# A streaming-encoder block on one core: both banded score products with 128 rows, and the final norm's roots in groups

## The chip, the core and the metric

The kernel runs on one core of a Trainium2 chip. The metric is device time in microseconds (us) from the start to the end of one execution. Engines: PE (TensorE, matmuls), DVE (VectorE), ACT (ScalarE), POOL (GpSimd) and SP (SyncE, which here only issues transfers). Each engine works through its own queue in order; SP, ACT and POOL also issue DMA transfers from their queues.

## What is computed

One layer on 1024 tokens of width 1024: an adaptive norm, a combined projection, two attention branches (latent attention, and banded attention of chunks of 64 tokens over their own and 8 earlier chunks), gates, an output projection, then a mixture of 32 experts (two per token) and a final norm. The parts that the change touches, cut from the reference:

```python
def rms_norm(x, g):
    y = xf * lax.rsqrt(jnp.mean(xf * xf, axis=-1, keepdims=True) + NORM_EPS)
    return y * g

def one_chunk(n):          # banded branch: 8 heads of 64, chunks of 64
    qc = q[n * 64 : n * 64 + 64]; kb, vb = the 9 chunks up to n
    sc = einsum('bqhd,bkhd->bhqk', qc, kb) * d ** -0.5 + bias
    p = softmax(where(valid, sc, NEG_INF))
    return einsum('bhqk,bkhd->bqhd', p, vb)
...
merged = sigmoid(gate_a) * (o_a @ w_oa) + sigmoid(gate_b) * (o_b @ w_ob)
x = x + gt1 * (merged @ w_out)
x = x + gt2 * hierarchical_moe(...)
return rms_norm(x, g_final)
```

## The kernel before

**Precision.** A float32 operand is split into a high part (rounded to the matmul format fp32r by a ScalarE copy) and a low part (the rest, by a DVE subtraction); `split`, lines 65 to 68. A product is then three matmuls, high x high, high x low, low x high (`mm3`, lines 70 to 74).

**Stages.** `front` (0 to some 206 us in the trace) norms, projects the latents and values, and stores the latent queries. `attend` runs 32 units of the banded branch, then 32 of the latent branch; `merge` blends the branches, projects out, routes the tokens; `experts` runs the experts and ends with the final norm.

**A unit** is one head and a group of two 128-token blocks (`unit`, from line 508). `soft` computes the scores of a block into PSUM (`st`, two buffers), adds the bias and takes the row minimum on DVE (L554), takes the exponential on ACT (L561), and scales by the reciprocal sum on POOL (L563). `trans` transposes the probabilities on PE (L578) and splits them; `value` multiplies by the values (L589, L590), adds the two halves through the tile o (L593, L594), splits the sum (L596, L597) and stores it. `pipeline` interleaves: unit i computes scores while unit i - 2 transposes and unit i - 3 multiplies by the values.

**Fill.** Between these steps a generator `fill` advances PE work of another kind. In the banded half that is `project`: a list of jobs, each 128 output columns of the combined projection for all 1024 tokens in 16 steps of three 512-column matmuls (two halves of 8 steps, an evacuation after each half). 33 steps run ahead of unit 0, then 10.8 with each unit (`BAND_RATE`). The list is pair 0 (queries, keys), pair 1, gates 0 to 3, pair 2, gates 4 to 7, pair 3, gates 8 to 15. A pair is two heads; units 8p to 8p + 7 belong to pair p, the even head (r = 0) in the first four for pairs 0 to 2.

**Banded scores.** `evac_q` puts the high part of a head's 64 query rows on one half of 128 partitions and the low part on the other (tile q). `evac_k` puts the high part of the keys on both halves (kd: L722 on ACT for one, L723 on POOL for the other) and the low part on the half of the head's own rows alone (kl, L724). So the first product (L785) has 128 rows and gives (high + low query) x high key, and the second one 64 rows:

```python
nc.tensor.matmul(out, it["q"][:, r, qs], it["kd"][:, r, ks], start=True, stop=False)
nc.tensor.matmul(out, it["q"][rr, r, qs], it["kl"][rr, ks], start=False, stop=True)
```

The latent branch takes its scores by `mm3` with 96 or 128 rows.

**Expert weights** come in loads of 1024 KB (tile we) on SP's queue; from the fourth on, each waits for the load two before it to have landed, and for its buffer (`weights`, L1292). Rows of ACT and DVE that split them are L67 and L68 with the tile whl.

**Pools.** s8 has 18 buffers of 8 KB per partition, s4 has 10 of 4 KB, s2 has 6 of 2 KB; t1 holds o and ohl.

**Final norm** (lines 1366 to 1392): g_final is loaded as one row, spread to 128 rows by matmuls with ones (L1371) and scaled on ACT (L1372). The residual rows are read back in eight tiles xz. For each, ACT squares with a row sum (L1385), DVE makes the root by a seed and three Newton steps on 128x1 (`rsqrt`, lines 76 to 92, eight small instructions), and the tile is multiplied by root and g_final on DVE (L1391); tiles 1 and 4 (`ASIDE`) by ACT (L1388) and POOL (L1389). SP stores it (L1392).

A scheduler puts the instructions of each engine in its queue, so their order is not quite that of the code.

## Time and profile before

| | us |
|---|---|
| median of 3 runs | 1348.7 (1345.55 to 1357.09) |
| the profiled execution | 1343.9 |
| its span, first to last instruction | 1342.2 |
| PE, DVE, ACT, POOL busy | 1216.0, 857.1, 642.4, 404.0 |

All times of rows are of the profiled execution, counted from its span's start. A matmul's end is modelled and overlaps the next one; what a matmul costs in a stream is read from start to start.

### The profile page before, as it was taken

To read this page: it belongs to the slowest core of one execution; us is meant where nothing else is said; L and a number is where in the kernel's file an instruction comes from. 1 tells how busy PE (TensorE), PEld (TensorE's weight loads), DVE (VectorE), ACT (ScalarE), POOL (GpSimd) and SP (SyncE) were. 2 spreads that over 40 slices of the span, in tenths; PEclk is the share of its full clock that TensorE was granted. 3 is DMA by queue.
4 is the path that set the end of the run, shared out by engine and by line. 5 is a ranking of instruction groups with operands and counts; after the bars stand their busy time and mean duration, and the time that the engine had idled before them with its cause. 6 is when DMAs were issued, how large, how long until landed. Compare 5 with 4: busy or idle time off the path is not lost. (4 is left out here: it accounts for less than half of the span.)

```text
span 1342.2 us, 17715 instructions
## 1 busy us (share of the span) xinstructions
PE 1216.0 (91%) x5866; PEld 958.7 (71%) x5866; DVE 857.1 (64%) x1761; ACT 642.4 (48%) x1271; POOL 404.0 (30%) x439
## 2 busy tenths in 40 slices
PE   4899969999999999999979999998599999998980
PEld 3787847677777777788869988887476776665640
DVE  7974525547556434367868872666787787875746
ACT  7453414334443344455667861312466565554533
POOL 3320203222222222222335755533323322322221
PEclk9899979999999999999989999999699999998995
DMA  9245791345355223389866574678589888999956
GB/s 370 90 127 187 214 294 61 104 143 190 93 165 179 69 84 118 126 271 313 256 202 194 173 223 160 234 299 330 179 278 292 295 294 295 304 317 321 311 180 258
DMA packets 103238, 288.36 MB, mean 215 GB/s; under 512 B 16629, under 2 KB 35189, under 8 KB 88776
## 3 DMA queue, kind: packets, MB, share of 16 engines
q1 hardware_dynamic: 85800, 247.32, 54.1%
q0 software_dynamic: 10288, 23.10, 6.9%
q10 hardware_dynamic: 7056, 16.78, 3.4%
q8 instruction: 47, 0.77, 0.2%
q14 instruction: 47, 0.39, 0.1%
HBM read 235.74 MB, written 68.17 MB: 226 GB/s over the span
## 5 line engine op out<-in xcount | busy, mean ns | idle before, releaser
L68 DVE TENSOR_TENSOR whl<-we,whl 128x1024 fp32r<-128x1024 f32 x125 | 150.6, 1222 | 49.8 <-ACT whl L67 46.7
L72 PE MATMUL bank<-hh,wx 128*128 128x512 f32 x384 | 159.1, 414 | 13.4 <-ACT wx L67 13.4
L563 POOL TENSOR_SCALAR pr<-pr,total 128x640 f32<-128x640 f32 (+7 forms) x128 | 96.1, 755 | 226.5 <-DVE total L562 189.7
L67 ACT CAST whl<-we 128x1024 fp32r<-128x1024 f32 x125 | 129.3, 1053 | 69.5 <-PE pp L74 53.2
L73 PE MATMUL bank<-hl,wx 128*128 128x512 f32 x384 | 152.3, 397 | 0.0
L74 PE MATMUL bank<-hh,wx 128*128 128x512 f32 x384 | 152.0, 397 | 0.0
L561 ACT ACTIVATE pr<-st,lowest 128x640 f32<-128x640 f32 (+7 forms) x128 | 89.8, 703 | 87.7 <-DVE lowest L554 51.3
L1396 POOL DMA_INDIRECT scratch_x<-eo,idx x32 | 57.7, 1803 | 213.9 <-DMA scratch_x<-eo,idx 72.8
L72 PE MATMUL pp<-whl,xh 128*128 128x512 f32 x256 | 113.3, 443 | 4.3 <-ACT whl L67 4.3
L1535 PE MATMUL pp<-we,hT 128*128 128x512 f32 x248 | 114.1, 602 | 0.8 <-ACT hT L1522 0.8
L68 DVE TENSOR_TENSOR pl<-bank,ph 128x512 fp32r<-128x512 f32 (+1 forms) x152 | 91.3, 613 | 32.1 <-ACT ph L67 28.2
L73 PE MATMUL pp<-whl,xh 128*128 128x512 f32 x256 | 104.8, 409 | 3.2 <-DVE whl L68 3.1
L74 PE MATMUL pp<-whl,xl 128*128 128x512 f32 x256 | 101.6, 397 | 0.0
L597 POOL TENSOR_TENSOR ohl<-o,ohl 64x256 fp32r<-64x256 f32 x64 | 54.4, 850 | 142.9 <-ACT ohl L596 92.8
L72 PEld LDWEIGHTS bank<-hh,wx 128*128 128x128 f32 x384 | 72.9, 190 | 33.0 <-ACT wx L67 13.8
L67 ACT CAST ph<-bank 128x512 fp32r<-128x512 f32 (+1 forms) x152 | 77.9, 530 | 36.3 <-PE bank L578 29.9
L74 PEld LDWEIGHTS bank<-hh,wx 128*128 128x128 f32 x384 | 72.7, 189 | 16.6 <-issue 0.5
L578 PE MATMUL bank<-ident,pr 128*128 128x128 f32 x528 | 82.8, 277 | 0.0
L73 PEld LDWEIGHTS bank<-hl,wx 128*128 128x128 f32 x384 | 73.2, 191 | 12.7 <-issue 0.2
L1535 PEld LDWEIGHTS pp<-we,hT 128*128 128x128 f32 x248 | 46.8, 193 | 48.1 <-issue 39.5
L554 DVE CUSTOM_DVE_ANT_0 st<-st,bias 128x640 f32<-128x640 f32 (+2 forms) x64 | 42.0, 666 | 49.0 <-PE st L786 48.8
L578 PEld LDWEIGHTS bank<-ident,pr 128*128 128x128 f32 x528 | 61.5, 142 | 5.5 <-issue 0.5
(380 smaller groups left out, 2905.1 us busy)
## 6 DMA issues: line engine op xcount, KB each, us to landing
we<-in_w_e SPq DMA_DIRECT2D x85, 1024.0 KB, 8.5
mw<-in_w_ada SPq DMA_DIRECT2D x64, 256.0 KB, 3.4
we<-in_w_e SPq DMA_DIRECT2D x17, 512.0 KB, 6.9
x<-in_x SPq DMA_DIRECT2D x16, 512.0 KB, 4.6
wada<-in_w_mod SPq DMA_DIRECT2D x8, 1024.0 KB, 8.9
w<-in_w_g SPq DMA_DIRECT2D x16, 512.0 KB
scratch_gate<-gs ACTq DMA_DIRECT2D x32, 256.0 KB, 3.0
gt<-scratch_gate SPq DMA_DIRECT2D x32, 256.0 KB, 2.9
```

What stands on the lines that cost most here:

```text
L67: nc.scalar.copy(hi, src)
L68: (eng or nc.vector).tensor_sub(lo, src, hi.bitcast(F32))
L72: mm(ps, lh, rh, start=start, stop=False)
L73: mm(ps, lh, rl, start=False, stop=False)
L74: mm(ps, ll, rh, start=False, stop=stop)
L554: nc.vector.tensor_tensor_reduce(sv, sv, bv, op0=OP.add, op1=OP.min, scale=1.0, scalar=3e38, accum_out=lowest)
L561: nc.scalar.activation(pv, sv, AF.Exp, bias=lowest, scale=-1.0, accum_out=total)
L563: nc.gpsimd.tensor_scalar(pr[:, 0:w], pr[:, 0:w], total, 1.0, op0=OP.mult, op1=OP.mult)
L578: nc.tensor.transpose(tp[:, i * P:(i + 1) * P], probs[s][:, lc:lc + P], self.ident)
L597: nc.gpsimd.tensor_sub(hl[rows, 1], o[rows, 1], hl[rows, 0].bitcast(F32))
L1396: self.nc.gpsimd.indirect_dma_start(out=self.scratch["x1"], out_offset=bass.IndirectOffsetOnAxis(ap=rows, axis=0), in_=o, in_offset=None, ...
L1535: nc.tensor.matmul(po[n], hT[:, ks], w[:, ns], start=k == 0, stop=k == 1)
```

## The change

Banded scores: the keys' low part gets a tile for each head of the pair, filled on both halves (the head's own by DVE, the other by a ScalarE copy, new L725), and the second product uses all 128 rows. It then also adds low query x low key. The even head's tile comes from t1 with one buffer, the odd head's from s4. The tile o shrinks to one half, one buffer, written in place. The list of jobs becomes pair 0, gates 0 and 1, pair 1, gates 2 to 5, pair 2, gates 6 to 8, pair 3, gates 9 to 15.

Final norm: g_final is read to 128 rows by one transfer into an s8 tile, ahead of the last expert's scatter in the code, and scaled on ACT. The squares of tiles 0 and 1, 2 to 4, 5 to 7 share one root chain each (eleven small instructions on 128x2 or 128x3), and all eight tiles are multiplied on DVE.

```diff
-ASIDE = (1, 4)
+FINAL = ((0, 2), (2, 5), (5, 8))
...
-            o = self.t1.tile([P, 2, 256], F32, name="o")
-            nc.scalar.copy(o[rows, 0], po[other, 0:256])
-            nc.vector.tensor_add(o[rows, 1], po[rows, 0:256], o[rows, 0])
+            o = self.t1.tile([P, 256], F32, name="o", bufs=1)
+            nc.scalar.copy(o[rows], po[other, 0:256])
+            nc.vector.tensor_add(o[rows], po[rows, 0:256], o[rows])
...
-                it["kl"] = self.t4([P, S], F32R, "kl")
+                it["kl"] = [self.t1.tile([P, S], F32R, name="kl", bufs=1), self.t4([P, S], F32R, "kl")]
...
-                    nc.vector.tensor_sub(kl[top, cs], pf[top], kd[top, r, cs].bitcast(F32))
+                    nc.vector.tensor_sub(kl[r][top, cs], pf[top], kd[top, r, cs].bitcast(F32))
+                    nc.scalar.copy(kl[r][low, cs], kl[r][top, cs].bitcast(F32))
...
-        jobs = pair_jobs(0)
-        for p in range(1, 4):
-            jobs += pair_jobs(p)
-            jobs += [gate(n) for n in range(4 * p - 4, 4 * p)]
-        jobs += [gate(n) for n in range(12, 16)]
+        jobs, gates = pair_jobs(0), iter(range(16))
+        for p, n in ((1, 2), (2, 4), (3, 3)):
+            jobs += [gate(next(gates)) for _ in range(n)] + pair_jobs(p)
+        jobs += [gate(n) for n in gates]
...
-                nc.tensor.matmul(out, it["q"][rr, r, qs], it["kl"][rr, ks], start=False, stop=True)
+                nc.tensor.matmul(out, it["q"][:, r, qs], it["kl"][r][:, ks], start=False, stop=True)
...
+        gf = self.t8([P, D], F32, "gf")
+        src = a["g_final"]
+        nc.sync.dma_start(gf, bass.AP(tensor=src.tensor, offset=src.offset, ap=[[0, P], [1, D]]))
         scatter(E - 1, self.down(self.turn_hidden(hid), lambda c: self.whole(E - 1, c)))
-        gf = self.t4([P, D], F32, "gf")
-        nc.sync.dma_start(gf[0:1], a["g_final"])
-        for n in range(2):
-            pb = self.pp()
-            nc.tensor.matmul(pb, self.ones[0:1], gf[0:1, n * HALF:(n + 1) * HALF], start=True, stop=True)
-            nc.scalar.activation(gf[:, n * HALF:(n + 1) * HALF], pb, AF.Copy, scale=RS)
+        nc.scalar.activation(gf, gf, AF.Copy, scale=RS)
...
+        for t0, t1 in FINAL:
+            for t in range(t0, t1):
+                junk = self.t4([P, D], F32, "junk")
+                nc.scalar.activation(junk, xs[t], AF.Square, accum_out=ss[:, t:t + 1])
+            self.rsqrt(self.small, rs[:, t0:t1], ss[:, t0:t1], t1 - t0, 1.0 / D)
         for t in range(NT):
...
-            if t in ASIDE:
-                nc.scalar.activation(x, x, AF.Copy, scale=rs)
-                nc.gpsimd.tensor_mul(x, x, gf)
-            else:
-                nc.vector.scalar_tensor_tensor(x, x, rs, gf, op0=OP.mult, op1=OP.mult)
-            nc.sync.dma_start(self.out[ts, :], x)
+            nc.vector.scalar_tensor_tensor(x, x, rs[:, t:t + 1], gf, op0=OP.mult, op1=OP.mult)
+            nc.sync.dma_start(self.out[t * P:(t + 1) * P, :], x)
```

What stands in the queues. ACT where pair 0's keys are evacuated, just ahead of the first unit (q, kd and kl are the pair's tiles, wx a weight block, pr the probabilities). Before:

```order
L714 ACTIVATE q<-bank 64x512
L722 CAST kd<-bank 64x512
L67 CAST wx<-w 128x1024
L722 CAST kd<-bank 64x512 x3
L561 ACT_TABLE_LOAD
L561 ACTIVATE pr,total<-st,lowest 128x128
L714 ACTIVATE q<-bank 64x512
L67 CAST wx<-w 128x1024
L561 ACTIVATE pr,total<-st,lowest 128x256
```

and now:

```order
L714 ACTIVATE q<-bank 64x512
L722 CAST kd<-bank 64x512
L67 CAST wx<-w 128x1024
L725 CAST kl<-kl 64x512
L722 CAST kd<-bank 64x512
L725 CAST kl<-kl 64x512
L722 CAST kd<-bank 64x512
L67 CAST wx<-w 128x1024
L725 CAST kl<-kl 64x512
L722 CAST kd<-bank 64x512
L561 ACT_TABLE_LOAD
L561 ACTIVATE pr,total<-st,lowest 128x128
```

The four copies into kl stand one behind each kd cast, the last of them behind the first exponential; the third weight block (wx) has moved ahead of it.

SP's queue around the load of g_final (gf), among the expert weights (we, with buffer numbers; we4 and we_more are halves of a load). Before:

```order
L1292 DMA we4_9317<-in_w_e 128x1024
L1292 DMA we_more_9318<-in_w_e 128x1024
L1292 DMA we_8596<-in_w_e 128x2048
L1292 DMA we_8598<-in_w_e 128x2048
L1368 DMA gf_11710<-in_g_final 1x1024
L1292 DMA we_8600<-in_w_e 128x2048
L1292 DMA we_8602<-in_w_e 128x2048
L1292 DMA we_8604<-in_w_e 128x2048
L1292 DMA we_8814<-in_w_e 128x2048
```

and now:

```order
L1291 DMA we4_9337<-in_w_e 128x1024
L1291 DMA we_more_9338<-in_w_e 128x1024
L1291 DMA we_8616<-in_w_e 128x2048
L1291 DMA we_8618<-in_w_e 128x2048
L1291 DMA we_8620<-in_w_e 128x2048
L1291 DMA we_8622<-in_w_e 128x2048
L1367 DMA gf_11712<-in_g_final 128x1024
L1291 DMA we_8624<-in_w_e 128x2048
L1291 DMA we_8834<-in_w_e 128x2048
```

The load of gf stands behind two more weight loads, and is 128 rows instead of one.

DVE at the start of the final norm (ss the sums of squares, rs the roots, rs_v, rs_i and rs_t the chain's tiles). Before:

```order
L82 TENSOR_SCALAR rs_v<-ss_11961 128x1
L83 TENSOR_SCALAR rs_i<-rs_v 128x1
L87 TENSOR_SCALAR rs_t<-rs_i,rs_v 128x1
L91 SCALAR_TENSOR_TENSOR rs_11962<-rs_t,rs_i 128x1
L87 TENSOR_SCALAR rs_t<-rs_11962,rs_v 128x1
L91 SCALAR_TENSOR_TENSOR rs_11962<-rs_t,rs_11962 128x1
L82 TENSOR_SCALAR rs_v<-ss_11978 128x1
L87 TENSOR_SCALAR rs_t<-rs_11962,rs_v 128x1
L83 TENSOR_SCALAR rs_i<-rs_v 128x1
L91 SCALAR_TENSOR_TENSOR rs_11962<-rs_t,rs_11962 128x1
L87 TENSOR_SCALAR rs_t<-rs_i,rs_v 128x1
L1391 SCALAR_TENSOR_TENSOR xz<-xz,rs_11962,gf 128x1024
```

and now:

```order
L82 TENSOR_SCALAR rs_v<-ss_11975 128x2
L83 TENSOR_SCALAR rs_i<-rs_v 128x2
L89 TENSOR_TENSOR rs_t<-rs_i 128x2
L90 TENSOR_TENSOR rs_t<-rs_t,rs_v 128x2
L91 SCALAR_TENSOR_TENSOR rs_11976<-rs_t,rs_i 128x2
L89 TENSOR_TENSOR rs_t<-rs_11976 128x2
L90 TENSOR_TENSOR rs_t<-rs_t,rs_v 128x2
L91 SCALAR_TENSOR_TENSOR rs_11976<-rs_t,rs_11976 128x2
L89 TENSOR_TENSOR rs_t<-rs_11976 128x2
L90 TENSOR_TENSOR rs_t<-rs_t,rs_v 128x2
L91 SCALAR_TENSOR_TENSOR rs_11976<-rs_t,rs_11976 128x2
L1385 SCALAR_TENSOR_TENSOR xz<-xz,rs_11976,gf 128x1024 x2
```

The chains of single tiles, woven into each other, are one chain of eleven for the first two tiles, and both multiplies follow it; the next group's chain stands behind them.

## Rows read from the trace of the kernel before

**Rows 1.** The page, part 1 (busy time of each engine, its share of the span, instructions) and the line of PE of part 2 (busy tenths in 40 equal slices).
```profile
PE 1216.0 (91%) x5866; PEld 958.7 (71%) x5866; DVE 857.1 (64%) x1761; ACT 642.4 (48%) x1271; POOL 404.0 (30%) x439
PE   4899969999999999999979999998599999998980
```
**Rows 2.** Busy time by stretch. Columns: stretch (us from the span's start) and its length, then busy us and instructions of PE, PEld, DVE, ACT and POOL, the granted clock of PE, the busy share of the DMA engines, GB/s.
```profile
206.00:575.00 369.00, 366.59 (x1722) 280.42 (x1721) 192.12 (x408) 154.10 (x333) 88.31 (x128) 1.00 0.39 123
...
1310.00:1342.00 32.00, 0.00 (x0) 0.00 (x0) 20.46 (x70) 11.28 (x18) 4.83 (x2) 0.50 0.70 265
```
**Rows 3.** What PE waited for from 206 to 575 us. Columns: engine, tile and line that waited, what it waited for; us in total, times, longest.
```profile
PE st L785 <- ACT pr L561: 2.2, 2, 1.7
PE bank L674 <- DVE macc L671: 0.2, 1, 0.2
```
**Rows 4.** The second score product (line 786): duration in ns (least, median, most), first and last start, and its shapes with their counts.
```profile
L786 PE MATMUL st<-kl,q x96: 323/410/500, 206.5 to 559.6; 64*128 64x320 f32 x64, 64*128 64x128 f32 x8, 64*128 64x384 f32 x8, 64*128 64x256 f32 x8
```
**Rows 5.** PE's timeline in one score call of 640 columns. Columns: start, us from start to modelled end, engine, line, operation, out<-in, rows*columns of the left operand, rows x columns of the moving operand, count.
```profile
423.09 0.39 PE L785 MATMUL st<-kd,q 128*128 128x320 f32 x1
423.42 0.41 PE L786 MATMUL st<-kl,q 64*128 64x320 f32 x1
423.76 0.41 PE L785 MATMUL st<-kd,q 128*128 128x320 f32 x1
424.10 0.41 PE L786 MATMUL st<-kl,q 64*128 64x320 f32 x1
424.44 0.50 PE L72 MATMUL bank<-hh,wx 128*128 128x512 f32 x1
424.78 0.40 PE L73 MATMUL bank<-hl,wx 128*128 128x512 f32 x1
425.01 0.39 PE L74 MATMUL bank<-hh,wx 128*128 128x512 f32 x1
```
**Rows 6.** PE's timeline, same columns, at two score products of the latent branch: 128 columns, and 320 columns behind transposes.
```profile
642.72 0.28 PE L73 MATMUL st<-kt,qt 96*128 96x128 f32 x1
642.83 0.27 PE L74 MATMUL st<-kt,qt 96*128 96x128 f32 x1
...
729.61 0.40 PE L72 MATMUL st<-kt,qt 96*128 96x320 f32 x1
729.84 0.31 PE L73 MATMUL st<-kt,qt 96*128 96x320 f32 x1
729.99 0.30 PE L74 MATMUL st<-kt,qt 96*128 96x320 f32 x1
730.13 0.31 PE L72 MATMUL st<-kt,qt 96*128 96x320 f32 x1
```
**Rows 7.** PE's timeline, same columns, in a banded score call of 128 columns.
```profile
430.01 0.22 PE L785 MATMUL st<-kd,q 128*128 128x128 f32 x1
430.16 0.32 PE L786 MATMUL st<-kl,q 64*128 64x128 f32 x1
430.41 0.50 PE L72 MATMUL bank<-hh,wx 128*128 128x512 f32 x1
430.75 0.39 PE L73 MATMUL bank<-hl,wx 128*128 128x512 f32 x1
```
**Rows 8.** Groups of instructions, from 200 to 575 us on ACT and DVE by form, and over the whole span on POOL (the page, part 5). Columns: line, engine, operation, out<-in, shapes, count | busy us, mean ns of one | idle us of the engine before them, and what ended most of it.
```profile
L722 ACT CAST kd<-bank 64x512 fp32r<-64x512 f32 x16 | 9.3, 581 | 29.1 <-PE bank L74 27.5 <-DVE kl L724 1.5
...
L724 DVE TENSOR_TENSOR kl<-bank,kd 64x512 fp32r<-64x512 f32 x16 | 11.0, 688 | 12.9 <-ACT kd L722 12.7
...
L597 POOL TENSOR_TENSOR ohl<-o,ohl 64x256 fp32r<-64x256 f32 x64 | 54.4, 850 | 142.9 <-ACT ohl L596 92.8
```
**Rows 9.** The wait of ACT's exp for DVE's row minimum, 206 to 575 us; columns as in group 3.
```profile
ACT pr L561 <- DVE lowest L554: 51.3, 26, 4.2
```
**Rows 10.** Timeline of SP's queue (issue of each load) and of DVE near the load of g_final.
```profile
1238.90 0.28 SPq L1368 DMA_DIRECT2D gf<-in_g_final  x1
1243.59 0.33 SPq L1292 DMA_DIRECT2D we<-in_w_e  x1
1246.79 0.33 SPq L1292 DMA_DIRECT2D we<-in_w_e  x1
...
1243.65 2.42 DVE L68 TENSOR_TENSOR whl<-we,whl 128x1024 fp32r<-128x1024 f32 x2
```
**Rows 11.** The largest wait of PE from 1208 to 1310 us; columns as in group 3.
```profile
PE pp L72 <- ACT whl L67: 4.3, 3, 2.0
```
**Rows 12.** Timeline of ACT, DVE and POOL in the final norm, in order of start.
```profile
1316.09 0.15 DVE L82 TENSOR_SCALAR rs_v<-ss 128x1 f32<-128x1 f32 x1 [10.89 <-ACT junk L1385]
1316.28 0.15 DVE L83 TENSOR_SCALAR rs_i<-rs_v 128x1 int32<-128x1 int32 x1
...
1322.46 0.19 ACT L1385 ACTIVATION_READ_ACCUMULATOR junk<-xz 128x1 f32 x1
...
1323.77 2.49 POOL L1389 TENSOR_TENSOR xz<-xz,gf 128x1024 f32<-128x1024 f32 x1 [16.73 <-ACT xz L1388]
1324.04 2.24 DVE L91 SCALAR_TENSOR_TENSOR rs<-rs_t,rs_i 128x1 f32<-128x1 f32 x1
...
1328.45 0.19 ACT L1385 ACTIVATION_READ_ACCUMULATOR junk<-xz 128x1 f32 x1
1336.74 1.28 DVE L1391 SCALAR_TENSOR_TENSOR xz<-xz,rs,gf 128x1024 f32<-128x1024 f32 x1
```

More of the change, by code (lines that the diff above doesn't have):

```diff
@@ L591, in value @@
             rows, other = (slice(0, 64), slice(64, 128)) if r == 0 else (slice(64, 128), slice(0, 64))
-            o = self.t1.tile([P, 2, 256], F32, name="o")
-            nc.scalar.copy(o[rows, 0], po[other, 0:256])
-            nc.vector.tensor_add(o[rows, 1], po[rows, 0:256], o[rows, 0])
+            o = self.t1.tile([P, 256], F32, name="o", bufs=1)
+            nc.scalar.copy(o[rows], po[other, 0:256])
+            nc.vector.tensor_add(o[rows], po[rows, 0:256], o[rows])
             hl = self.t1.tile([P, 2, 256], F32R, name="ohl")
-            nc.scalar.copy(hl[rows, 0], o[rows, 1])
-            nc.gpsimd.tensor_sub(hl[rows, 1], o[rows, 1], hl[rows, 0].bitcast(F32))
+            nc.scalar.copy(hl[rows, 0], o[rows])
+            nc.gpsimd.tensor_sub(hl[rows, 1], o[rows], hl[rows, 0].bitcast(F32))
             nc.sync.dma_start(o_dst[rows, :, g * 256:(g + 1) * 256], hl[rows].bitcast(F32))
@@ L776, in band_unit @@
                 next(mods, None)
-            rr = slice(64 * r, 64 * r + 64)
             if i == 28:
@@ L1378, in experts @@
             nc.sync.dma_start(xs[t], self.scratch["x1"][t * P:(t + 1) * P, :])
+        ss = self.small.tile([P, NT], F32, name="ss8")
+        rs = self.small.tile([P, NT], F32, name="rs8")
+        for t0, t1 in FINAL:
[3 more added lines that the diff above has]
+            self.rsqrt(self.small, rs[:, t0:t1], ss[:, t0:t1], t1 - t0, 1.0 / D)
         for t in range(NT):
-            ts = slice(t * P, (t + 1) * P)
             x = xs[t]
-            junk = self.t4([P, D], F32, "junk")
-            ss = self.small.tile([P, 1], F32, name="ss1")
-            rs = self.small.tile([P, 1], F32, name="rs1")
-            nc.scalar.activation(junk, x, AF.Square, accum_out=ss)
-            self.rsqrt(self.small, rs, ss, 1, 1.0 / D)
-            if t in ASIDE:
-                nc.scalar.activation(x, x, AF.Copy, scale=rs)
-                nc.gpsimd.tensor_mul(x, x, gf)
-            else:
-                nc.vector.scalar_tensor_tensor(x, x, rs, gf, op0=OP.mult, op1=OP.mult)
-            nc.sync.dma_start(self.out[ts, :], x)
+            nc.vector.scalar_tensor_tensor(x, x, rs[:, t:t + 1], gf, op0=OP.mult, op1=OP.mult)
+            nc.sync.dma_start(self.out[t * P:(t + 1) * P, :], x)
     def add_rows(self, o, rows):
```

## The prediction, made before the changed kernel ran

> **What bounds the kernel now.** I read the page first: TensorE (PE) is busy for 91% of the span, next comes VectorE (DVE) with 64% [rows 1]. Busy time of PE is modelled, so I looked at the stretch that the first half of the change touches, the banded scores with the projections beside them, from 206 to 575 us: PE 366.6 of 369.0 us, its granted clock 1.00 (2.4 GHz), while DVE has 192.1, ScalarE (ACT) 154.1 and the DMA engines 39% [rows 2]. The waits of PE there come to 2.4 us in all [rows 3]. So PE's own stream is the bound: what an instruction takes from its start to the next start is path, and other engines wait for PE. The last stretch, 1310 to 1342 us, has no PE work at all [rows 2]; it is the final norm, where DVE is the busiest engine.
>
> **The second score product.** A pair of products (L785 with 128 rows, L786 with 64) makes up to 512 score columns; there are 96 pairs, 64 of them 320 columns wide, 8 each of 128, 256 and 384 [rows 4], and the 8 left have 512. A 640-column score row is two pairs in a call, 32 calls; the other 32 calls have one pair. In the timeline of one wide call the starts are 423.09, 423.42, 423.76, 424.10, then the following projection at 424.44 and the next at 424.78: 1.69 us for four score products and one follower [rows 5]. The follower is itself late: 0.34 us from start to start, and 0.23 for the next like it (424.78 to 425.01). The control is the latent-attention score product of the same width with 96 rows: 0.23 us for the first behind transposes, then 0.15 and 0.14 [rows 6]. Five starts at control prices are 0.23 + 3 x 0.145 + 0.23 = 0.90 us, so a wide call pays 1.69 - 0.90 = 0.79 us for its 64-row instructions, and 32 calls 25.3 us. The change gives every product 128 rows with the same columns and the same left operand, so I take all of it as gone.
>
> For a single pair the nearest rows give two ends. With 128 columns it is 430.01 to 430.75, 0.74 us for two products and their follower [rows 7]; at 0.11 us each [rows 6] and 0.23 for the follower it would be 0.45, a saving of 0.29. The last pair of the wide call, 423.76 to 424.78, is 1.02 against 2 x 0.145 + 0.23 = 0.52, a saving of 0.50 [rows 5, 6]. Widths lie between and most have another matmul ahead, so I take 0.38: 32 x 0.38 = 12.2 us (9.3 to 16.0). Together 37.5 us, with ends of 34 and 41.
>
> That 96 rows cost nothing and 64 do is what these rows show. The Trainium skill agrees in "TensorEngine Tiling (Array Packing)", Key Properties: changing the tiling mode, not just the tile, drains TensorE. Another page of it, "TensorE: Matmul & The Clock Gate", in its closing table (Why this matters for your kernels), says that a single product with few rows takes as long as one with 128; by that rule alone the widening saves nothing, and the sum would end near 1342. The trace speaks for the drain, since the follower with 128 rows is late as well. I keep the other as the second rival.
>
> **What the wider product costs elsewhere.** The second half of the low part is filled by a ScalarE copy (new L725), 16 in all, as many as the kd casts, which take 581 ns each [rows 8]: 9.3 us on an engine with 154 of 369 us busy [rows 2]. Each waits for the DVE subtraction ahead of it (688 ns [rows 8]), and exps and casts queue behind it. ACT already waits 51.3 us for DVE minima in this stretch, up to 4.2 at a time [rows 9], and of that PE saw 2.2 us [rows 3]; so the copies are covered. Because PE's stream gets a tenth shorter, I add 2.4 us for new waits, as much again as the present ones; the ends are 0 and half of the gain, 18 us.
>
> **Later pairs and the single buffer.** The low part of even heads now has one buffer, so a pair's key evacuation waits for the last even-head scores of the pair before. By the code 33 steps of fill precede unit 0 and 10.8 go with each unit; pair 1's key job is now the sixth, its first half ends at step 88, in unit (88 - 33) / 10.8 = 5.1; pair 0's even heads are done after unit 3. Pair 3's key job is the seventeenth: unit 21.4 against 20, and complete at 22.1, before unit 24 reads it. The margin is over a unit each time, and a unit is 369 / 32 = 11.5 us [rows 2]. Jobs only swap places, so PE's total is the same. Cost 0. The partial output o loses its second buffer; its reader is a GpSimd (POOL) subtraction of 850 ns [rows 8], far under a unit. Cost 0; if it showed, it would be in the latent units, by at most that much for each of 32, and on ACT first.
>
> **g_final.** It was a 4 KB load and two broadcasts on PE; now it is a 128-row load of 512 KB into a large buffer, on SP's queue between the expert weights. As built, it waits for the second weight split of the first large block behind we_more, four loads ahead of it in the queue; the corresponding split of before ends at 1243.65 + 2.42 = 1246.1 [rows 10]. The load of before (1238.90) stood two weight loads earlier. With two more weight loads ahead, the next weight load would be due at 1246.79 by its own pace [rows 10], so the wait itself hides in the pace. Its bytes do not: loads follow each other by 3.2 us there [rows 10], and each is 1,024 KB, so 512 KB push the last eleven loads by 1.6 us, and PE waits for split weights at that end already (4.3 us [rows 11]). I charge 1.6 us (0 to 3). Its scaling is one more ACT instruction over a tile, on an engine that waits for the loads there; cost 0.
>
> **The final norm.** Before, the last multiply starts at 1336.74 and ends at 1338.02; DVE is the chain. One of its tiny steps lasts 2.24 us instead of 0.15, beside a GpSimd multiply of 2.49 us that starts at 1323.77 [rows 12]; there are two such multiplies. After, the roots of tiles 2 to 4 start when the fifth square is read, 1322.65; eleven steps of 0.19 us (1316.09 to 1316.28) are 2.1, three multiplies of 1.28 are 3.8: 1328.6. The last group starts at 1328.64, when the eighth square is read, and takes 2.1 + 3.8: 1334.5 [rows 12]. That is 3.5 us earlier. Ends: 4.5 if the eighth tile lands earlier, 0 if the stores hold the end.
>
> **Sum.** From the profiled execution, 1343.9 us: - 25.3 - 12.2 + 2.4 + 1.6 - 3.5 = 1306.9 us, a saving of 37.0. The median of the runs shown is 4.8 us above the profiled execution, so I forecast 1312.
>
> **Rivals.**
> *The gain comes back as waits* (chance 0.15). With PE quicker, the chain scores, DVE minimum, exp, and the two score buffers end last, and half of the gain is lost: 1312 + 18 = 1330. For it: 26 waits of ACT for the minimum, up to 4.2 us [rows 9]. Against: PE saw only 2.2 us of them.
> *Rows do not matter* (0.05). The step between starts is a price of these products, not of 64 rows: nothing in the band, - 3.5 + 1.6 at the end: 1347. Against: the follower's 0.34.
> *g_final holds the weight queue* (0.06). If the split it waits for comes one expert later, three loads of 3.2 us or some 10 us [rows 10], eleven loads are late and PE, which waits for them already, loses it: 1322. Against: the timeline just worked out.
> *Slower: ScalarE's in-order queue* (0.04). Each of 16 copies sits at the head of ACT while DVE works off what stands before its subtraction. Should every one cost the longest wait seen, 4.2 us [rows 9], plus 0.58 itself, and PE feel it all, that is 76 us: 1312 + 76 = 1388. It decides from 37.0 / 16 = 2.3 us per copy on PE's path. Against: PE's share of ACT's present waits.
>
> **How the numbers follow.** The forecast holds 0.70. A measurement here tells about 1% from no change. Faster by more than that means under 1335: the forecast, the g_final case and most of the first rival, 0.90. Within 1%: the rows rival and a little of the others, 0.07. Slower: 0.03. The range takes the unknown costs at their good ends below (41 in the band, 4.5 in the norm, no waits, no charge for g_final: 1303, and a little for the offset between runs) and reaches to the first rival above: 1300 to 1331.
>
> **What would show it.** Right: a wide call from its first score product to the follower's successor in 0.9 us instead of 1.69, all score products with 128 rows, PE waits in the band still a few us, the band some 35 us shorter, the later stages shifted whole; the last multiply some 3.5 us sooner behind the loads of the tiles, no 2.24 us step. Wrong: starts still 0.34 apart; or PE waits for ACT or DVE of 10 us and more in the band; or a gap in the weight loads around g_final.

## The result, and the profile of the changed kernel

The changed kernel takes 1314.97 us (median of 4, 1306.83 to 1317.16) against 1347.49 (median of 4) on the same chip: a ratio of 0.9743, 95% interval 0.9701 to 0.9784. Run once more beside the last experiments it took 1312.52 against 1348.39, ratio 0.9723 (0.9666 to 0.9781). So the change saves 33 to 36 us (32.5 and 35.9); the forecast was 1312. Its profiled execution took 1314.96 us, span 1313.2.

The page after, part 1, beside [rows 1]:

```profile
PE 1178.8 (90%) x5862; PEld 952.3 (73%) x5862; DVE 856.1 (65%) x1732; ACT 648.3 (49%) x1284; POOL 391.2 (30%) x437
```

PE has 37.2 us less of busy time for nearly as many instructions. By stretch (columns as in [rows 2]): the banded half from the first banded score to the last projection product, and the final norm.

```profile
200.80:539.80 339.00, 336.41 (x1763) 281.33 (x1762) 198.76 (x421) 164.54 (x352) 88.07 (x130) 1.00 0.46 146
1282.00:1313.00 31.00, 0.00 (x0) 0.00 (x0) 15.13 (x41) 9.20 (x16) 0.00 (x0) 0.50 0.77 282
```

The same band of the kernel before runs from 206.4 to 582.0 us, 375.6. It is now 36.6 us shorter with PE's clock at 1.00 in both, and PE is still busy for all but 2.6 us of it. Its waits there, beside [rows 3]:

```profile
PE bank L72 <- DVE pl L68: 1.4, 1, 1.4
PE bank L72 <- DVE lowest L554: 0.7, 1, 0.7
PE bank L578 <- DVE q L715: 0.5, 1, 0.5
```

The second product (now line 785; [rows 4] has its old form), then PE's timeline at a wide call and at one with 128 and 384 columns, beside [rows 5] and [rows 7]:

```profile
L785 PE MATMUL st<-kl,q x96: 273/309/477, 200.8 to 517.6; 128*128 128x320 f32 x64, 128*128 128x128 f32 x8, 128*128 128x384 f32 x8, 128*128 128x256 f32 x8
```

```profile
309.15 0.39 PE L784 MATMUL st<-kd,q 128*128 128x320 f32 x1
309.38 0.31 PE L785 MATMUL st<-kl,q 128*128 128x320 f32 x1
309.53 0.31 PE L784 MATMUL st<-kd,q 128*128 128x320 f32 x1
309.68 0.31 PE L785 MATMUL st<-kl,q 128*128 128x320 f32 x1
309.82 0.39 PE L72 MATMUL bank<-hh,wx 128*128 128x512 f32 x1
310.05 0.40 PE L73 MATMUL bank<-hl,wx 128*128 128x512 f32 x1
...
321.86 0.31 PE L784 MATMUL st<-kd,q 128*128 128x128 f32 x1
322.01 0.27 PE L785 MATMUL st<-kl,q 128*128 128x128 f32 x1
322.12 0.39 PE L784 MATMUL st<-kd,q 128*128 128x384 f32 x1
```

From 309.15 to 310.05 is 0.90 us, where [rows 5] have 1.69. The follower at 309.82 is on time: the next starts 0.23 us behind it.

ACT's new copies (group from 195 to 540 us; columns as in [rows 8]) and ACT's wait for the row minimum, which was 51.3 us [rows 9]:

```profile
L725 ACT CAST kl<-kl 64x512 fp32r<-64x512 f32 x16 | 9.9, 620 | 7.7 <-DVE kl L724 7.6
...
ACT pr L561 <- DVE lowest L554: 45.0, 28, 3.2
```

SP's queue at g_final (timeline, as in [rows 10]), and what PE waited for at that end of the experts, 1180 to 1276 us, beside [rows 11]:

```profile
1201.08 11.79 SPq L1291 DMA_DIRECT2D we<-in_w_e  x4
1221.17 0.33 SPq L1367 DMA_DIRECT2D gf<-in_g_final  x1
1221.55 15.39 SPq L1291 DMA_DIRECT2D we<-in_w_e  x5
```

```profile
PE pp L72 <- ACT whl L67: 3.4, 2, 2.0
```

The load of g_final waited 8.2 us in the queue for its buffer, so there is a gap in the weight loads ahead of it: the last one in front was issued at 1212.55, the next at 1221.55. Five follow, two of them at once and the others 3.6 to 6.7 us apart. PE waited no longer for split weights than before. Last, the final norm, beside [rows 12]: the eighth square read, the last group's first step, the last three multiplies.

```profile
1301.23 0.19 ACT L1381 ACTIVATION_READ_ACCUMULATOR junk<-xz 128x1 f32 x1
...
1303.04 0.16 DVE L82 TENSOR_SCALAR rs_v<-ss 128x3 f32<-128x3 f32 x1
...
1305.20 3.68 DVE L1385 SCALAR_TENSOR_TENSOR xz<-xz,rs,gf 128x1024 f32<-128x1024 f32 x3
```

### The profile page after: what moved, and what is told of

Read it like the earlier page. It is cut to its first block, busy times and chain, and to the rows that moved or that the text cites. A ratio compares the mean times of both kernels' runs of the same rounds, so it can differ in the third digit from the quotient of the medians.

```text
span 1313.2 us, 17638 instructions
## 1 busy us (share of the span) xinstructions
PE 1178.8 (90%) x5862; PEld 952.3 (73%) x5862; DVE 856.1 (65%) x1732; ACT 648.3 (49%) x1284; POOL 391.2 (30%) x437
## 4 chain that ended last, share of the span: by engine, by line
PE 52%; DMA 29%; DVE 10%; issue 5%; ACT 3%; SPq 1%; POOL 1%; POOLq 0%; DVEq 0%; ACTq 0%
DMA scratch_x<-eo,idx 21%; PE bank L72 10%; PE bank L73 10%; PE bank L74 10%; PE bank L578 3%; PE pp L72 2%; PE pp L73 2%; PE pp L74 2%; PE bank L590 2%; PE bank L589 2%; DMA X<-scratch_h,idx 2%; PE st L72 1%; DVE acc L325 1%; PE st L73 1%; PE st L74 1%
## 5 line engine op out<-in xcount | busy, mean ns | idle before, releaser
L72 PE MATMUL bank<-hh,wx 128*128 128x512 f32 x384 | 155.5, 405 | 11.7 <-ACT wx L67 10.3
L74 PE MATMUL bank<-hh,wx 128*128 128x512 f32 x384 | 151.3, 395 | 0.0
L68 DVE TENSOR_TENSOR pl<-bank,ph 128x512 fp32r<-128x512 f32 (+1 forms) x152 | 91.1, 612 | 23.0 <-ACT ph L67 21.2
L597 POOL TENSOR_TENSOR ohl<-o,ohl 64x256 fp32r<-64x256 f32 x64 | 51.1, 799 | 136.9 <-ACT ohl L596 90.4
L73 PEld LDWEIGHTS pp<-whl,xh 128*128 128x128 f32 x256 | 48.9, 191 | 21.3 <-DVE whl L68 8.8
```

The lines of the kernel that those rows point to most:

```text
L68: (eng or nc.vector).tensor_sub(lo, src, hi.bitcast(F32))
L72: mm(ps, lh, rh, start=start, stop=False)
L73: mm(ps, lh, rl, start=False, stop=False)
L74: mm(ps, ll, rh, start=False, stop=stop)
L597: nc.gpsimd.tensor_sub(hl[rows, 1], o[rows], hl[rows, 0].bitcast(F32))
```

## The experiments

Median times, and four stretches of each profiled execution. "Band" is from the first banded score to the last projection product (the first of the three matmuls of the last step); "rest" from there to the issue of the first tile load of the norm; "norm" from there to the start of the last multiply. All in us; the stretches are differences of starts rounded to 0.1, so they can be 0.1 off. The medians come from different chips, on which before takes 1347 to 1354, so two kernels are compared by their ratios to before on their own chip.

| kernel | median | first score | band | rest | norm |
|---|---|---|---|---|---|
| before | 1347 to 1354 | 206.4 | 375.6 | 729.6 | 25.1 |
| changed | 1314.97 | 200.8 | 339.0 | 746.3 | 21.5 |
| changed, again | 1312.52 | 203.3 | 340.5 | 744.2 | 21.1 |
| band only | 1313.84 | 201.3 | 340.1 | 738.6 | 25.1 |
| norm only | 1349.33 | 205.6 | 376.8 | 735.3 | 21.6 |
| order only | 1347.31 | 202.2 | 371.4 | 740.5 | 23.9 |
| rows, old order | 1320.24 | 205.1 | 343.9 | 736.7 | 24.9 |
| sorted call | 1336.52 | 205.3 | 363.8 | 732.5 | 25.0 |
| 96 rows | 1310.97 (one) | 203.7 | 340.9 | 737.6 | 21.3 |
| copy on POOL | 1313.08 | 203.1 | 341.5 | 740.4 | 21.1 |
| small g_final | 1310.90 | 200.7 | 339.6 | 735.0 | 21.4 |
| no POOL multiply | 1351.72 (one) | 203.6 | 375.7 | 742.7 | 22.5 |
| groups with POOL | 1355.10 (one) | 207.8 | 375.6 | 739.7 | 24.6 |
| wide mod product | 1308.11 | 203.9 | 338.5 | 742.4 | 21.2 |

### Which half brings it: band only, norm only

The kernel before with the banded lines of the change's diff, and with those of its final norm. The line of each that matters most:

```diff
+nc.tensor.matmul(out, it["q"][:, r, qs], it["kl"][r][:, ks], ...)     # band only, with tiles, copies, order
+FINAL = ((0, 2), (2, 5), (5, 8))                                      # norm only, with g_final's load
```

> The whole banded part of the change on the kernel before (both score products with 128 rows, two low-part tiles, the other order of the jobs, one buffer for o), with the final norm as before. Theory (the time comes from the score products): some 30 us faster than before, about 1317, ratio about 0.978; from the first banded score to the last projection product about 339 us where before has 375.6; in the final norm 25.1 us from the issue of the first tile load to the start of the last multiply, as before. Rival (the norm and its load bring a good part): less than 25 us faster.

> The final norm's part alone on the kernel before (the 512 KB load of g_final among the expert weights, roots in groups, no GpSimd multiply), the banded scores as before. Theory: 21.5 us from the issue of the first tile load to the start of the last multiply where before has 25.1, and the weight loads behind g_final's 0 to 2 us later: 1 to 3 us faster, within 1% of before. Rival (g_final's load holds the queue of the weight loads): a gap of 5 us and more ahead of it in the weight loads that PE feels, same time or slower.

The banded half alone has a ratio to before of 0.9734 (0.9694 to 0.9773), the norm alone 0.9999 (0.997 to 1.003). As expected, the time comes from the band: 340.1 us, with the norm at the old 25.1. The norm's part does what it was to do in its own stretch (21.6), and no gap in the weight loads shows in the time, but 1 to 3 us of gain cannot be told from none.

### What in a product costs: sorted call, 96 rows

```diff
 for c in range(parts):        # before: both products of a pair, then the next pair
-    scores(...)
+    scores(..., 0)            # 128 rows
+for c in range(parts if bias is not None else 0):
+    scores(..., 1)            # 64 rows
```

> The kernel before with its 64-row second products, but where a call has two pairs, both 128-row products come first and both 64-row products behind them, so that PE goes from one row count to the other twice in a wide call and not four times. Theory (the change of the row count costs, some 0.2 us each): a wide call with its follower takes about 1.3 us where before has 1.69, 32 calls save about 12 us, about 1336. Rival (a 64-row product is slow by itself, by whatever order): nothing saved, 1348. A third way (the wait is at every product into the same bank behind another): nothing saved, and starts still 0.34 apart inside the sorted call.

Ratio 0.9903 (0.9869 to 0.9938), 13 us, with the same instructions in another order. PE's timeline in a sorted wide call (columns as in [rows 5]; L789 the 128-row, L791 the 64-row product):

```profile
415.09 0.54 PE L789 MATMUL st<-kd,q 128*128 128x320 f32 x2
415.56 0.56 PE L791 MATMUL st<-kl,q 64*128 64x320 f32 x2
416.05 0.51 PE L72 MATMUL bank<-hh,wx 128*128 128x512 f32 x1
416.39 0.39 PE L73 MATMUL bank<-hl,wx 128*128 128x512 f32 x1
```

From 415.09 to 416.39 is 1.30 us. With none of the changes between 128 and 64 rows it is 0.90, with two of them 1.30, with four 1.69: 0.20 us for each change, and nothing for the 64 rows by themselves. The rivals fall: the product slow by itself, since two 64-row products are still in the call, and the bank, since the changed kernel goes through the same banks in the same order with starts 0.15 us apart.

```diff
-nc.tensor.matmul(out, it["q"][:, r, qs], it["kl"][r][:, ks], ...)
+rr = slice(0, 96 if r == 0 else 128)
+nc.tensor.matmul(out, it["q"][rr, r, qs], it["kl"][r][rr, ks], ...)
```

> The changed kernel, but in even heads the second score product takes 96 of the 128 rows (it leaves out half of the product of the two low parts there), in odd heads 128: so that in even heads PE changes the row count, from 128 to 96 and back, as often as in the kernel before. Theory (64 rows are another way of working for PE, 96 are not): starts 0.15 us apart at 320 columns in even heads as in odd ones, the follower 0.23, band 339 us. Rival (every change of the row count costs): starts 0.34 apart in even heads, band some 18 us longer. Second rival (the cost goes by the rows left out): something between, 8 to 10 us.

```profile
312.33 0.40 PE L784 MATMUL st<-kd,q 128*128 128x320 f32 x1
312.56 0.31 PE L786 MATMUL st<-kl,q 96*128 96x320 f32 x1
312.71 0.31 PE L784 MATMUL st<-kd,q 128*128 128x320 f32 x1
312.86 0.31 PE L786 MATMUL st<-kl,q 96*128 96x320 f32 x1
313.00 0.39 PE L72 MATMUL bank<-hh,wx 128*128 128x512 f32 x1
313.23 0.40 PE L73 MATMUL bank<-hl,wx 128*128 128x512 f32 x1
```

Going from 128 rows to 96 and back costs nothing: 0.90 us again. It is 64 that is another way of working. Where the 0.2 us lie shows in the loads of the left operands, which the trace lists by themselves (PEld, 0.18 to 0.19 us each). The load for the 128-row product that starts at 423.76 before [rows 5], and for the one at 309.53 in the changed kernel:

```profile
423.75 0.19 PEld L785 LDWEIGHTS st<-kd,q 128*128 128x128 f32 x1 [0.16 <-issue]
```

```profile
309.38 0.19 PEld L784 LDWEIGHTS st<-kd,q 128*128 128x128 f32 x1
```

Changed, the load starts 0.15 us ahead of its product, beside the product in front; before, it starts with its own product. So do the loads of all 96 of the 64-row products of before, and in the sorted kernel that of the first one in each of the 64 calls. The second one of a sorted wide call has its load 0.14 us ahead, and a 96-row product above 0.15 (312.41 against 312.56). So at a change between 128 and 64 rows the load of the left operand no longer lies beside the product in front, and the price is about as long as the load. Why the load waits is not shown.

This fits the rule of the Trainium skill in "TensorEngine Tiling (Array Packing)", Key Properties, that a change of the tiling mode drains TensorE; this case puts 0.2 us beside it. Going by the closing table of "TensorE: Matmul & The Clock Gate" of the Trainium skill (Why this matters for your kernels) alone, a lone product with few rows takes as long as a full one: true here for two 64-row products in a row (two changes and four changes, at 0.20 us each, explain 1.30 and 1.69 us and leave nothing for the rows), and no help where they alternate with 128.

### Rows and order apart: order only, rows with the old order

```diff
+for p, n in ((1, 2), (2, 4), (3, 3)):                                 # order only: as in the change
+    jobs += [gate(next(gates)) for _ in range(n)] + pair_jobs(p)
```

```diff
-it["kl"] = self.t4([P, S], F32R, "kl")                                # rows, old order
+it["kl"] = [self.t4([P, S], F32R, "kl"), self.t4([P, S], F32R, "kl")]
...
+nc.scalar.copy(kl[r][low, cs], kl[r][top, cs].bitcast(F32))
...
-nc.tensor.matmul(out, it["q"][rr, r, qs], it["kl"][rr, ks], ...)
+nc.tensor.matmul(out, it["q"][:, r, qs], it["kl"][r][:, ks], ...)
```

> Only the other order of the projection jobs (pairs later among the gates), the products, tiles and norm as before. Theory: the order does nothing to the length of the band (about 375 us from the first banded score to the last projection product), and it is what takes 5.6 us out of the stretch ahead of the first score, since jobs of the front change places: about 1342, ratio about 0.996. Rival: the front is as before (first score at 206), so that the 5.6 us come with the new tiles; then no change. Second rival: the later key jobs shorten the band themselves, by 5 us or more.

> The kernel before with 128 rows in both score products (the low parts of even and odd heads both in 4 KB buffers), but with its old order of the jobs, two buffers for o and its old final norm. Theory (each change of the row count costs PE some 0.18 to 0.2 us, of which the band had 192): the first score stays at 206 us and the band from the first score to the last projection product takes 339 to 342 us, so nearly all of the band's gain comes without the order, and the time is some 33 us under before, about 1316. Rival (order and rows add up, as the order alone brought 4.2 us in the band): 344 us for the band, about 1320. Second rival (without the later pairs the low parts find no free buffer): PE waits of 10 us and more for key evacuations in the band.

Both went another way than I had expected. The order alone has a ratio of 0.9965 (0.9936 to 0.9994), and takes 4.2 us from the band as well as from the front; the rows alone leave the band at 343.9, the rival's number, ratio 0.9758 (0.9701 to 0.9815). What PE waited for in the band of the rows with the old order:

```profile
PE bank L674 <- DVE macc L671: 3.0, 2, 2.9
PE bank L72 <- DVE lowest L554: 1.4, 1, 1.4
PE st L786 <- ACT pr L561: 1.0, 1, 1.0
...
```

With three shorter ones (0.6, 0.5 and 0.3) that is 6.8 us where before has 2.4. Without waits PE's stream is 375.6 - 2.4 = 373.2 us before, 343.9 - 6.8 = 337.1 with the rows alone, 339.0 - 2.6 = 336.4 in the changed kernel. So the rows are worth 36.1 us of PE's stream, 0.19 for each of the 192 changes of the row count; with the old order 4.4 of them come back as waits, and the new order keeps most of those away. No key evacuation was among the waits, so the second rival fell. The 4.4 are from one profile on either side, and the changed kernel's 2.6 us of waits is the least of the seven profiles with the new order and the wider products, which have 2.6 to 4.7, mean 3.8; so what the new order keeps away is 2 to 4 us. The order-only kernel has but 0.2 us of waits; 2.0 us of its gain in the band are in PE's starts, and what they are stays open.

The front: with the old order the first score starts at 203.6 to 207.8 us (six profiles, mean 205.6), with the new one at 200.7 to 203.9 (eight, mean 202.4). The trace shows where: before, SP's queue issues four more loads for the modulation rows (mw) ahead of a weight of the latent queries (wq) than now, seven against three. SP's timeline, before and then changed, in a view that starts at 90 us and so shows the last five and the last one of them:

```profile
92.89 5.10 SPq L667 DMA_DIRECT2D mw<-in_w_ada  x5
98.09 0.37 SPq L231 DMA_DIRECT2D wq<-in_w_uq  x1
```

```profile
92.30 0.33 SPq L667 DMA_DIRECT2D mw<-in_w_ada  x1
92.73 0.37 SPq L231 DMA_DIRECT2D wq<-in_w_uq  x1
```

The order-only kernel issues wq at 93.07, also behind one load of mw in that view. That these 5 us are what comes out at the first score was not tried by itself.

### ScalarE's copies: copy on POOL

```diff
-nc.scalar.copy(kl[r][low, cs], kl[r][top, cs].bitcast(F32))
+nc.gpsimd.tensor_copy(kl[r][low, cs], kl[r][top, cs])
```

> The changed kernel with the low part's second half copied by GpSimd in place of ScalarE, 16 copies. Theory (the copies lie beside other work on either engine): the band stays at 339 us within 2, and the time at that of the changed kernel, 1311 to 1317. Rival (ScalarE's queue is on PE's path): the band shorter by 3 us and more. Third way (GpSimd's copies are late for the scores of the pair): PE waits for the low part, band longer by 3 us and more.

Band 341.5 and 1313.08 us, 2.5 us over the first profile of the changed kernel and 1.0 over the second; no wait of PE in the band is for the keys' low part, and in the changed kernel no instruction is listed as waiting for a copy. So the copies cost nothing that shows on either engine, and the rival in which ScalarE's queue makes the kernel slower falls.

### The load of g_final, and the wide modulation product

```diff
-gf = self.t8([P, D], F32, "gf")            # small g_final: as in the kernel before, behind the last scatter
-nc.sync.dma_start(gf, ...ap=[[0, P], [1, D]])
+gf = self.t4([P, D], F32, "gf")
+nc.sync.dma_start(gf[0:1], a["g_final"])
+...                                        # and the two matmuls with ones
```

> The changed kernel with the old 4 KB load of g_final and its two broadcasts on PE behind the last expert, the roots in groups. Theory (512 KB among the weights cost PE at most the 1.6 us of their bytes): 0 to 2 us quicker from the first expert's transposes to the last expert product, and the broadcasts put 1 to 2 us back ahead of the tile loads: the same time as the changed kernel, 1311 to 1317. Rival (the large load holds the weight queue): the expert stage 5 us shorter than the 350 us of the changed kernel and the time about 1309.

```diff
-nc.tensor.matmul(pr[0:1], self.ones[:, 0:1], acc, start=True, stop=True)
+nc.tensor.matmul(pr, self.ones, acc, start=True, stop=True)
```

(with the small load of g_final)

> The changed kernel with the old small load of g_final, and the eight products of the modulation rows with 128 equal left columns in place of one (two instructions each; the instruction behind them in the changed kernel is 0.34 us from the next, not 0.23). Theory (a change of the column count costs PE as one of the row count does): the instruction behind these products is on time, 0.23 us from start to start at 512 columns, the one ahead 0.15 and not 0.24 at 320, and the band 1 to 3 us shorter, 337 us. Rival (the lateness there is that of another number format or place): no difference in the starts. The time is that of the changed kernel within its noise, 1308 to 1316.

> The changed kernel once more, beside the variant with the small load of g_final and the wide modulation products on the same chip. Theory (the spread of its runs comes from the gathers ahead of the experts and not from the change): 1311 to 1317 as median; from the first expert's transposes to the last expert product 344 to 352 us, the longer the more PE waits for gathers (7 us at the lower, 14 at the upper end). Rival (the 512 KB load costs the expert stage): the variant 3 us and more quicker in the expert stage at equal waits for gathers.

The small load: ratio to before 0.9699 (0.9643 to 0.9754), within the noise of the changed kernel's 0.9743. From the first expert's transposes to the last expert product its profile has 344.8 us, the changed kernel 350.1 and 357.0. That looks like the rival; but the kernels with the small load spread from 342.6 to 355.0 there (nine profiles, mean 348.7), those with the large one from 349.6 to 357.0 (five, mean 351.8). PE's wait for gathered token rows goes the same way: 4.9 to 16.4 us with the small load, 10.0 to 14.0 with the large one. In the changed kernel:

```profile
PE pp L1484 <- DMA X<-scratch_h,idx: 14.0, 6, 5.0
```

Of the kernels with the small load, order only has 11.4 us of it and the one without POOL multiplies 16.4, though neither touches the experts. Nor does the wait explain every run: the 357.0 of the changed kernel's second profile come with 12.1, outside the 352 that I had expected as the upper end, and the wide mod kernel has 352.4 us with 4.9. What g_final's 512 KB cost, 0 to 3 us, stays open.

The wide modulation product, PE's timeline from the last score on, and the same place of the changed kernel's second profile:

```profile
221.68 0.31 PE L785 MATMUL st<-kl,q 128*128 128x320 f32 x1
221.83 1.02 PE L674 MATMUL bank<-macc,ones 128*128 128x512 f32 x2
222.29 0.79 PE L72 MATMUL bank<-hh,wx 128*128 128x512 f32 x1
222.92 0.39 PE L73 MATMUL bank<-hl,wx 128*128 128x512 f32 x1
```

```profile
221.09 0.31 PE L785 MATMUL st<-kl,q 128*128 128x320 f32 x1
221.33 1.02 PE L674 MATMUL bank<-macc,ones 128*1 128x512 f32 x2
222.28 0.50 PE L72 MATMUL bank<-hh,wx 128*128 128x512 f32 x1
222.61 0.39 PE L73 MATMUL bank<-hl,wx 128*128 128x512 f32 x1
```

Half right. From the score ahead to the follower's successor it is 1.24 us and not 1.52, 0.28 less; at the eight such places it is 0.24 to 0.29. The band is 2.0 us shorter than in the second profile of the changed kernel, and 0.5 than in the first. The product starts on time, 0.15 us behind the score, but the follower is later (0.63, not 0.23). So the product with one left column costs more than one with 128, some 0.09 us ahead of it and 0.19 behind, and the theory that the follower would be on time fell: it is late behind a product with 128 columns too, which means that a late follower alone is no sign of a change of row or column count. The median of 1308.11 is the lowest of all; its ratio to before, 0.9685 (0.9621 to 0.9749), overlaps that of the changed kernel on the same chip, 0.9723 (0.9666 to 0.9781). That it beats the changed kernel isn't shown.

### The norm: no POOL multiply, groups with POOL

```diff
-ASIDE = (1, 4)                             # no POOL multiply: the kernel before
+ASIDE = ()
```

```diff
+self.rsqrt(self.small, rs[:, t0:t1], ss[:, t0:t1], t1 - t0, 1.0 / D)   # groups with POOL: the kernel before,
+if t in ASIDE:                                                         # roots as in the change
+    nc.scalar.activation(x, x, AF.Copy, scale=rs[:, t:t + 1])
+    nc.gpsimd.tensor_mul(x, x, gf)
```

> The kernel before with all eight final multiplies on VectorE and none on GpSimd, roots still tile by tile. It tells apart what of the norm's 3.6 us comes from leaving GpSimd out. Theory (VectorE's chain is slowed by GpSimd's two multiplies, some 2.1 us each, and two multiplies of 1.28 us come to it): 23.5 us from the issue of the first tile load to the start of the last multiply, where before has 25.1 and the changed kernel 21.5. Rival (the roots of each tile fill VectorE, GpSimd only relieved it): 27 us and more.

> The kernel before with the roots in three groups, but tiles 1 and 4 still multiplied by GpSimd. Theory (the groups bring the gain, since the last root starts when the eighth square is read): 21.5 to 22 us from the issue of the first tile load to the start of the last multiply, as in the changed kernel. Rival (a GpSimd multiply beside VectorE's small steps takes some 2 us back): 23.5 us and a small step of 2 us in the last two groups.

22.5 us without the POOL multiplies, under the 23.5 expected; 24.6 with the groups and POOL, so the groups by themselves bring only 0.5 of 25.1, and the theory of the second kernel fell. Leaving POOL out brings 2.6, the groups on top of it 0.9 to 1.4. The reason, in the timeline of POOL and DVE with groups and POOL:

```profile
1334.15 2.35 POOL L1391 TENSOR_TENSOR xz<-xz,gf 128x1024 f32<-128x1024 f32 x1 [15.89 <-ACT xz L1390]
...
1335.14 1.40 DVE L82 TENSOR_SCALAR rs_v<-ss 128x3 f32<-128x3 f32 x1 [2.76 <-ACT junk L1384]
...
1338.55 2.48 DVE L1393 SCALAR_TENSOR_TENSOR xz<-xz,rs,gf 128x1024 f32<-128x1024 f32 x2
...
1339.83 3.39 POOL L1391 TENSOR_TENSOR xz<-xz,gf 128x1024 f32<-128x1024 f32 x1 [3.32 <-ACT xz L1390]
...
1340.94 2.31 DVE L82 TENSOR_SCALAR rs_v<-ss 128x3 f32<-128x3 f32 x1
```

A DVE step of 0.17 us ends with the POOL multiply that it met: 1335.14 + 1.40 = 1336.54 against 1334.15 + 2.35 = 1336.50, and 1343.25 against 1343.22. In [rows 12] it is 1324.04 + 2.24 = 1326.28 against 1323.77 + 2.49 = 1326.26. The other way round POOL's second multiply takes 3.39 us where the first took 2.35, having started during a DVE multiply. "SBUF — State Buffer" of the Trainium skill (Who interferes with whom) says that VectorE and GpSimd share a port pair, and that where both need it the first to come holds it for its whole instruction; these rows agree.

## Why the prediction was right, point by point

**PE's stream is the bound of the band: right.** It is still busy for all but 2.6 us of 339.0.

**The rows, - 37.5: right, a little large.** 36.1 us by the rows alone, 36.8 in the changed kernel. The price per call came out to the hundredth: 0.90 us forecast and measured for a wide call, from the control [rows 6]. The cause, forecast as the change between row counts and not the rows, is shown by the sorted call and the 96 rows; the late follower, by which the prediction argued for it, would not have been enough, as the wide modulation product has one without any such change.

**New waits, + 2.4: about right.** PE's waits went from 2.4 to 2.6 in the first profile, so + 0.2, but to 4.1 in the second, and to 3.8 in the mean of the seven profiles with this band, so + 1.4. The forecast's reason (a shorter stream meets more waits) holds; with the old order they grew by 4.4. What it left out is the next point.

**The order of the jobs at 0: wrong.** "Jobs only swap places, so PE's total is the same" forgot that an order also sets who waits. It keeps 2 to 4 us of waits out of the band, and moves four modulation loads away from the front's weights; the first score comes 3.2 us sooner in the mean of the profiles, 5.6 in the two compared here. The later pairs and the low part's single buffer, on the other hand, cost nothing: no wait for a key evacuation is in the rows of the changed kernel.

**The single buffer of o at 0: shows on ACT.** The prediction named the place, the latent units, and the engine. There ACT's copy into o (L593) waits for the GpSimd subtraction that still reads it:

```profile
ACT o L593 <- POOL ohl L597: 2.1, 2, 1.3
```

All seven profiles with one buffer have 2.1 to 2.2 us of this wait, the seven with two have none. From the last projection product to the last product with latent values it is 220.1 us in the mean of the former and 218.2 of the latter, with 216 to 224 in single profiles; whether PE pays for the wait is not shown.

**ACT's copies at 0: right**, by the copy on POOL, and by the trace, where nothing waits for them.

**g_final, + 1.6: open.** Its buffer came free 8.2 us after its turn in the queue (5.3 to 12.8 in the five profiles with this load), and not within the pace of 3.2 us as forecast. So the gap in the weight loads, which the prediction had named as a sign of being wrong, is there; yet PE's wait for split weights is 3.4 us, not above the 4.3 of before [rows 11]. The times bound the whole norm part to ±4 us, no closer.

**The norm, - 3.5: right (- 3.6)**, and for the reason that was named. The last group waits for DVE's multiplies (1303.04), not for the eighth square (1301.42): the two had been forecast within 0.1 us.

**The sum.** By the profiled executions the saving is 1343.93 - 1314.96 = 29.0 us, and not 37.0: - 5.6 in the front, - 36.6 in the band, + 16.7 in the rest, - 3.6 in the norm, 0.1 behind it. The rest has the same work on either side but for the buffer of o and g_final's bytes. Before's 729.6 us there are the least of the fourteen profiles, whose others lie between 732.5 and 746.3, mean 739.4; so 9.8 of the 16.7 us are the luck of that one execution. Medians don't hang on one execution, and they give 33 to 36 us. But the parts at their own places come to more: 36.6 in the band, 3.2 in the front by the means, 3.6 in the norm, 43.4 together. So some 7 to 11 us of it come back behind the band by the medians as well. The eight profiles with the widened product have 740.2 us there in the mean, the six with 64 rows 736.7; how much of that is the change's and how much scatter stays open. That 1312 came within 3 us of the median is thus in part luck: the forecast had neither the gain in the front nor the longer rest, and the two in part cancel.

## What to carry to other kernels

Read matmuls from start to start, follower included, and look where the loads of the left operands start: a load that starts with its product, not ahead of it, marks the change here. A control of the same width elsewhere in the trace prices it before anything is built; that it is the change and not the product itself took the sorted call to show. If products with few rows can't be avoided, put those of one row count together, and where spare rows can hold something useful or a copy, fill them. An order of jobs that leaves an engine's work alone still moves its neighbours' transfers and waits: go through the queues ahead of the first step that moved, too.

## What the runs showed that was not expected

- A change between 128 and 64 rows costs PE 0.19 to 0.20 us (36.1 us for 192; 0.79 for four in a wide call), one between 128 and 96 nothing. At a change to or from 64 rows the left operand's load starts with its product, otherwise some 0.15 us ahead.
- Two-instruction products with one left column cost 0.24 to 0.29 us more than with 128.
- A GpSimd multiply of 2.35 us holds a 0.17-us DVE step until its own end, and is itself held by a DVE multiply that started ahead of it.
- With nearly the same work, the stretch behind the band varies from 729.6 to 746.3 us between executions (729.6 to 742.7 with the band's products as before), and PE's waits for gathered rows from 4.9 to 16.4 us.
